# Down projection with VectorE and ScalarE in written order, PSUM banks of even and odd pairs exchanged, and PSUM emptied directly behind each tile

## The chip, the cores and the metric

The kernel runs on one core of one Trainium2 chip. Its time is device microseconds from launch to end; lower is better. One profiled execution gives the trace that is read here. Engines: TensorE (PE in the rows, its weight loads PEld) multiplies matrices into PSUM, VectorE (DVE) and ScalarE (ACT) do elementwise work, GpSimd (POOL) and SyncE (SP) issue transfers, which the DMA engines carry out.

## The reference, cut to what matters

One decoder layer in fp32 on 512 tokens of width 2048: four mixers, an output projection, then the gated MLP and a last norm. The change lies in the MLP's second product, the down projection:

```python
def conv_gated_mlp(h, w_up, w_dw, b_dw, w_down):
    up = h @ w_up
    gate, val = jnp.split(up, 2, axis=-1)
    gate = causal_dwconv(gate, w_dw, b_dw)
    return (jax.nn.gelu(gate, approximate=True) * val) @ w_down
...
        x = x + conv_gated_mlp(h, ffn_w_up[l], ffn_w_dw[l], ffn_b_dw[l], ffn_w_down[l])
    return rmsnorm(x, norm_final_g)
```

`w_down` is 5504 x 2048, so the inner dimension is 43 slices of 128 and the output 16 tiles of 128 columns (d = 0 to 15) by 512 tokens.

## The kernel before, in words

Every fp32 operand is split into a high part `hi` (a ScalarE cast to fp32r) and a low part `lo` (a VectorE subtraction, raw minus hi); a product is two or three matmuls of these parts. So a weight block can be multiplied only after a DMA, a ScalarE cast and a VectorE subtraction, in that order.

`down` works through the 43 slices in four stages, and `down_end` does the last five slices and the norm.

- **Straight stages**, `eights(0)` and `eights(2)`, five slices each. The 16 output tiles are done in two halves of eight (`sw`), and a half takes all eight PSUM banks: tiles d = 0 to 3 in `pb`, d = 4 to 7 in `pa`. One weight chunk (a slice by eight tiles) gives 8 x 3 matmuls. `chunk` stages a chunk's split two chunks ahead (three buffers each for hi and lo). With each of the first seven chunks `forms_dn` prepares, for the next stage, one pair of activation slices (tile `ap`, two buffers, read back from DRAM): three casts on ScalarE, three subtractions and four combinations on VectorE, the last cast waiting for the combinations. After a half the eight banks are emptied: copied to `xn` (stage 0) or added to it (stage 2). The next half needs the banks.
- **Paired stages**, `seven(0)` and `seven(1)`, fourteen slices each, by Winograd's scheme: two by two blocks take seven products instead of eight. For each pair j of output tiles (j and j + 8) there are the products a, r1, r2, b, r3, d, r4 of 14 matmuls, in the order a(j), d(j-1), r1(j), r4(j-1), r2(j), b(j), r3(j). The weight sums r1 and r3 come from an accumulating DMA on POOL. r2 and r4 are made on VectorE in place (r2 = r1 + a, r4 = r2 + b), and only then cast and subtracted. `product` accumulates several forms into one bank (a, r2, r3 and d; r1 and r4), and after every form VectorE adds the bank's two halves to `xn` (two adds of 256 columns). A bank's next form waits for the adds of the form before it. The split of product k + 2 (`stage`) stands in the code ahead of product k and its adds.

What sets the order: TensorE runs in the order of the code. SP and POOL, and before the change VectorE and ScalarE too, are ordered by a scheduler that walks a timeline of its own and lets work of `high_priority` go ahead of other ready work. Each engine then runs its list in order, and an instruction that waits holds up all behind it. `tails` threads the next stage's first loads and splits (`sa`, the activations of a straight stage; `raw`, `hi` and `lo` of its first chunks) into the last seven products.

Of the kernel before, what the change touches and what calls it, by code (L numbers as in the profile page):

```python
# [8 lines left out]
F32 = mybir.dt.float32  # L9
# [4 lines left out]
ADD, SUB, MUL = ALU.add, ALU.subtract, ALU.mult  # L14

P = 128
D = 2048
S = 512
# [31 lines left out]
class Kernel:  # L50
# [1004 lines left out]
    def tail(self):  # L1055
        tc = self.tc
        self.mp.release()
        self.ap.release()
        fx = tc.alloc_tile_pool(name="fx", bufs=1, reuse_waits="tile")
        ft = tc.alloc_tile_pool(name="ft", bufs=1, reuse_waits="tile")  # L1060
        ft2 = tc.alloc_tile_pool(name="ft2", bufs=2, reuse_waits="tile")
        self.x2d = [self.dr.tile([P, 1024], F32, name=f"x2d{p}") for p in range(8)]
        self.tp = ft
        self.acc = self.tmp("rstd", pool=self.cp)
        self.xf = []
        for q in range(4):
            ps = self.quad(q, (0, 2), 0)
            for o in range(4):
                x = self.x2[4 * q + o]
                self.tt(x, x, ps[o], ADD)  # L1070
            for p in (2 * q, 2 * q + 1):
                self.forms1(fx, p)
            for p in (2 * q, 2 * q + 1):
                self.square2(p, ft2)
        self.ffn_std()
        ft2.release()
        ft.release()
        ub = tc.alloc_tile_pool(name="ub", bufs=1, reuse_waits="tile")
        self.ffn_up(self.xf, self.rp, self.rs, ub)
        for pool in (ub, fx, self.aq, self.rp):  # L1080
            pool.release()
        self.rp = tc.alloc_tile_pool(name="rp2", bufs=8, side="right", reuse_waits="tile")
        self.xp = tc.alloc_tile_pool(name="xp", bufs=1, reuse_waits="tile")
        self.fx = tc.alloc_tile_pool(name="fx2", bufs=1, reuse_waits="tile")
        self.ft = tc.alloc_tile_pool(name="ft3", bufs=2, reuse_waits="tile")
        self.down()
        for pool in (self.ft, self.fx):
            pool.release()
        with tc.tile_pool(name="dp", bufs=1, reuse_waits="tile") as dp, \
                tc.tile_pool(name="dp2", bufs=2, reuse_waits="tile") as dp2, \  # L1090
                tc.tile_pool(name="dq", bufs=5, reuse_waits="tile") as self.endq:
            self.tp = dp
            base_tmp = self.tmp
            self.tmp = lambda tag, w=512, dt=F32, pool=None: base_tmp(tag, w, dt, pool or (dp2 if tag == "sq" else None))
            self.down_end()
        for pool in (self.xp, self.rp):
            pool.release()
# [256 lines left out]
    def eights(self, i):  # L1354
        nc, n = self.nc, DN[i + 1] - DN[i]
        forms = list(range(NP2))
        self.xf = []
        step = 0
        for sw in range(2):
            ps = [self.pb() if d < 4 else self.pa() for d in range(8)]  # L1360
            for k in range(n):
                wh, wl = self.chunk()
                if i == sw == 0 and k in (0, 2):
                    self.sacts(i, k + 2, min(k + 4, n))
                for d in range(8):
                    c = slice(d * P, d * P + P)
                    self.mm3(ps[d], wh[:, c], wl[:, c], self.sa[k][:, 0], self.sa[k][:, 1], k == 0, k == n - 1)
                step += 1
                if forms:
                    self.forms_dn(forms.pop(0), DN[i + 1])  # L1370
                if 2 * n - 3 <= step < 2 * n:
                    yield step
            for d in range(8):
                if i == 0:
                    x = self.xp.tile([P, S], F32, tag=f"x{8 * sw + d}", name=f"xn{8 * sw + d}")
                    self.x2.append(x)
                    with self.tc.high_priority(self.hp):
                        nc.scalar.copy(x, ps[d])
                    continue
                x = self.x2[8 * sw + d]  # L1380
                with self.tc.high_priority(self.hp):
                    self.tt(x, x, ps[d], ADD)

    def resid2(self, d):
        x = self.x2d[d // 2][:, 512 * (d % 2):512 * (d % 2) + 512]
# [22 lines left out]
    def seven(self, g):  # L1408
        tc, nc, a = self.tc, self.nc, self.a
        W = NP2 * P  # L1410
        IX = {"a": 0, "b": 1, "r4": 2, "r1": 3, "r3": 4, "d": 5, "r2": 6}
        seq = [(0, x) for x in ("a", "r1", "r2", "b", "r3")]
        for j in range(1, 9):
            for form, back in (("a", 0), ("d", 1), ("r1", 0), ("r4", 1), ("r2", 0), ("b", 0), ("r3", 0)):
                if j - back < 8:
                    seq.append((j - back, form))
        raws, staged, bank = {}, {}, {}
        blk = lambda j, x: a["w_dns"][g, j + 8 * (x in "cd"), :, int(x in "bd")]

        def load(k):  # L1420
            if k >= len(seq):
                return
            j, form = seq[k]
            if form in ("r2", "r4"):
                return
            t = (self.wp if form == "d" else self.rp).tile([P, 1024], F32, tag="raw", name=f"d{form}{g}_{j}")[:, 0:W]
            raws[j, form] = t
            nc.sync.dma_start(t, blk(j, "c" if form in ("r1", "r3") else form))
            if form in ("r1", "r3"):
                nc.gpsimd.dma_start(t, blk(j, "d" if form == "r1" else "a"), accum_op=ADD)  # L1430

        def stage(k):
            if k >= len(seq):
                return
            j, form = seq[k]
            if form in ("r2", "r4"):
                t = raws[j, "r1"]
                self.tt(t, t, raws[j, "a" if form == "r2" else "b"], ADD)
                raws[j, form] = t
            hi = self.wq.tile([P, 1024], F32R, tag="hi", name=f"dh{form}{g}_{j}")[:, 0:W]  # L1440
            lo = self.wq.tile([P, 1024], F32R, tag="lo", name=f"dl{form}{g}_{j}")[:, 0:W]
            self.split_to(hi, lo, raws[j, form])
            staged[k] = (hi, lo)

        def product(k):
            j, form = seq[k]
            wh, wl = staged.pop(k)
            new = form in ("a", "b", "r1")
            if new:
                bank[j, form] = self.pa() if form == "b" else self.pb() if j % 2 else self.pa()  # L1450
            ps = bank[j, {"r2": "a", "r3": "a", "d": "a", "r4": "r1"}.get(form, form)]
            for p in range(NP2):
                x, c = self.xf[p][:, IX[form]], slice(p * P, p * P + P)
                self.mm(ps, wh[:, c], x.rearrange("p n c->p (n c)"), new and p == 0, False, True)
                self.mm(ps[:, 256:512], wl[:, c], x[:, 0], False, p == NP2 - 1, True)
            up, half, op = {"a": (0, 0, ADD), "b": (0, 0, ADD), "r2": (0, 1, ADD), "r4": (0, 1, ADD),
                            "r3": (8, 1, SUB), "r1": (8, 1, SUB), "d": (8, 0, SUB)}[form]
            x = self.x2[j + up][:, 256 * half:256 * half + 256]
            with tc.high_priority(self.hp if k > len(seq) - 4 else 0):
                for i in range(2):  # L1460
                    self.tt(x, x, ps[:, 256 * i:256 * i + 256], op)

        LD, AH = 6, 2
        for k in range(LD):
            with tc.high_priority(self.hp):
                load(k)
        yield None
        for k in range(AH):
            with tc.high_priority(self.hp):
                stage(k)  # L1470
            yield None
        for k in range(len(seq)):
            with tc.high_priority(self.hp):
                load(k + LD)
                stage(k + AH)
            product(k)
            if g == 0 and seq[k][1] == "r3" and seq[k][0] < 6:
                self.resid2(seq[k][0] + 2)
                self.resid2(seq[k][0] + 10)
            yield len(seq) - 1 - k  # L1480
# [139 lines left out]
```

## Time and profile before

| | us |
|---|---|
| median of 3 runs | 1883.13 |
| lowest, highest | 1864.03, 1888.47 |
| the profiled execution | 1867.63 |
| its span, first to last instruction | 1865.8 |
| TensorE busy | 1814.8 (97%) |
| VectorE busy | 1580.3 (85%) |
| ScalarE busy | 908.0 (49%) |

The down projection starts at 1394 us of the span: the first straight stage to 1450, the first paired stage to 1593, the second straight stage to 1655, the second paired stage to 1794, then the end stage. In the rows of a timeline the first number is the start in us, the second the duration; `x2` is two instructions in a row; what stands in brackets is the idle time before it and what ended that. In a list of waits come the total in us, how often, and the longest. Buffer numbers are left out there: `dr` is a raw weight tile of r1 or r3 (and, summed in place, of r2 and r4), `dhr` and `dlr` its high and low part, `da`, `db`, `dd` the tiles of a, b, d; `ap` and `Y` are the activations of a paired stage and their forms.

### The profile page before, as it was taken

Reading aid. Unit: us, or ns where it says so; the run is one execution under the profiler, and the core shown is the slowest. Engines: PE = TensorE matmul, PEld = TensorE weight load, DVE = VectorE, ACT = ScalarE, POOL = GpSimd, SP = SyncE. Lnnn points to the kernel's source line nnn. Section 1 sums busy time; section 2 is a strip of 40 time slices with the busy share of each in tenths; the row PEclk is TensorE's granted clock in tenths of the full one; section 3 lists DMA queues with packets and bytes.
Section 4 is the critical chain, followed back from the end, with each engine's and each line's share of the span. In section 5 each row is a group of like instructions: output and inputs, shape, how many; then the busy total and the mean of one; then the engine's idle time right before and its main releaser. Section 6 shows DMA issues by size and latency. Waiting matters only on the chain.

```text
span 1865.8 us, 26091 instructions
## 1 busy us (share of the span) xinstructions
PE 1814.8 (97%) x9670; PEld 1546.8 (83%) x9670; DVE 1580.3 (85%) x2392; ACT 908.0 (49%) x1188; POOL 208.0 (11%) x291
## 2 busy tenths in 40 slices
PE   8899999999899999999999999999999999899997
PEld 6788887888788888888888888888888788788886
DVE  8699989998695788888888888888887889778975
ACT  6332446533484455555555555555555434433444
POOL 6210020202000100000000000000001210000000
PEclk9999999999999999999999999999999999999998
DMA  5322322423244877777777777777749985577632
GB/s 201 100 88 93 105 94 93 164 80 96 91 167 141 229 212 196 205 202 204 211 194 205 204 202 212 197 206 200 204 120 266 259 209 153 161 213 191 163 99 94
DMA packets 111728, 313.58 MB, mean 168 GB/s; under 512 B 15792, under 2 KB 21936, under 8 KB 111600
## 3 DMA queue, kind: packets, MB, share of 16 engines
q1 hardware_dynamic: 91776, 249.25, 39.6%
q0 software_dynamic: 19536, 62.14, 19.8%
q8 instruction: 76, 1.25, 0.3%
q10 hardware_dynamic: 288, 0.52, 0.1%
q14 instruction: 52, 0.43, 0.1%
HBM read 289.71 MB, written 19.66 MB: 166 GB/s over the span
## 4 chain that ended last, share of the span: by engine, by line
PE 84%; DVE 8%; DMA 4%; ACT 3%; issue 1%; POOL 0%; DVEq 0%; SPq 0%; ACTq 0%; POOLq 0%
PE pa L97 55%; PE pb L97 29%; DVE lo L60 2%; DMA ap<-act 1%; DMA raw<-w_dn 1%; ACT hi L106 1%; DMA ur<-w_up 1%; DVE X L60 1%; DVE M L60 0%; DVE Y L60 0%; DVE A L63 0%; DMA raw<-w_a 0%; DVE bk L60 0%; DVE xn L60 0%; DMA av<-act 0%
## 5 line engine op out<-in xcount | busy, mean ns | idle before, releaser
L97 PE MATMUL pa<-A,hi 128*128 128x512 f32 x1312 | 415.1, 399 | 15.1 <-ACT A L73 7.4
L97 PEld LDWEIGHTS pa<-A,hi 128*128 128x128 f32 x1312 | 247.9, 191 | 75.2 <-ACT A L73 7.8
L106 ACT CAST uhr<-ur 128x1024 fp32r<-128x1024 f32 x160 | 167.9, 1050 | 217.4 <-PE pb L97 112.6
L97 PE MATMUL pa<-A,lo 128*128 128x512 f32 x656 | 258.7, 398 | 2.7 <-DVE lo L60 2.7
L106 ACT CAST hi<-raw 128x1024 fp32r<-128x1024 f32 (+1 forms) x127 | 132.3, 1043 | 219.0 <-PE pa L97 166.4
L60 DVE TENSOR_TENSOR ulr<-ur,uhr 128x1024 fp32r<-128x1024 f32 x160 | 195.8, 1224 | 45.5 <-ACT uhr L106 41.7
L97 PE MATMUL pb<-X,uhr 128*128 128x512 f32 x640 | 225.5, 391 | 1.2 <-ACT uhr L106 1.2
L97 PE MATMUL pa<-X,uhr 128*128 128x512 f32 x640 | 225.4, 391 | 0.0
L60 DVE TENSOR_TENSOR lo<-raw,hi 128x1024 fp32r<-128x1024 f32 (+1 forms) x127 | 157.4, 1241 | 52.4 <-ACT hi L106 51.8
L97 PE MATMUL pb<-X,ulr 128*128 128x256 f32 x640 | 179.3, 280 | 0.8 <-DVE ulr L60 0.8
L97 PE MATMUL pa<-X,ulr 128*128 128x256 f32 x640 | 179.2, 280 | 0.0
L1225 POOL DMA_DIRECT2D ur<-w_up x80 | 69.9, 874 | 802.7 <-DMA ur<-w_up 497.5
L97 PEld LDWEIGHTS pa<-A,lo 128*128 128x128 f32 x656 | 124.6, 190 | 32.1 <-DVE lo L60 3.6
L97 PEld LDWEIGHTS pb<-X,uhr 128*128 128x128 f32 x640 | 119.7, 187 | 27.7 <-ACT uhr L106 1.5
L97 PEld LDWEIGHTS pa<-X,uhr 128*128 128x128 f32 x640 | 119.7, 187 | 26.2
L97 PEld LDWEIGHTS pb<-X,ulr 128*128 128x128 f32 x640 | 121.0, 189 | 1.1 <-DVE ulr L60 1.1
L97 PEld LDWEIGHTS pa<-X,ulr 128*128 128x128 f32 x640 | 121.0, 189 | 0.0
L97 PE MATMUL pa<-X,uhb 128*128 128x512 f32 x320 | 112.7, 391 | 0.0
L106 ACT CAST dhr<-dr 128x896 fp32r<-128x896 f32 x64 | 60.4, 943 | 98.9 <-PE pa L97 51.0
L97 PE MATMUL pa<-X,ulb 128*128 128x256 f32 x320 | 89.6, 280 | 0.0
L63 DVE SCALAR_TENSOR_TENSOR M<-h,par,M 128x511 f32<-128x511 f32 (+29 forms) x120 | 85.7, 747 | 0.1
L97 PE MATMUL pb<-sa,hi 128*128 128x512 f32 (+1 forms) x280 | 77.3, 362 | 4.0 <-DVE xn L60 3.8
(346 smaller groups left out, 4211.6 us busy)
## 6 DMA issues: line engine op xcount, KB each, us to landing
ur<-w_up SPq DMA_DIRECT2D x80, 512.0 KB, 7.7
ur<-w_up POOLq DMA_DIRECT2D x80, 512.0 KB, 7.9
raw<-w_b SPq DMA_DIRECT2D x40, 512.0 KB, 3.7
ud<-w_up SPq DMA_DIRECT2D x40, 512.0 KB, 9.0
ua<-w_up SPq DMA_DIRECT2D x40, 512.0 KB, 7.3
ub<-w_up SPq DMA_DIRECT2D x40, 512.0 KB, 4.3
raw<-w_out SPq DMA_DIRECT2D x32, 512.0 KB, 3.6
dr<-w_dns SPq DMA_DIRECT2D x32, 448.0 KB, 4.1
```

Of the source, the lines that this page charges most:

```text
L60: (eng or self.nc.vector).tensor_tensor(out, x, y, op=op)
L63: self.nc.vector.scalar_tensor_tensor(out, x, s, y, op0=op0, op1=op1)
L97: self.nc.tensor.matmul(ps, lhsT=l, rhs=r, start=start, stop=stop, skip_group_check=go_on)
L106: self.nc.scalar.copy(hi, src)
L1225: nc.gpsimd.dma_start(v8(t), blk(f, "d" if form == "r1" else "a"), accum_op=ADD)
```

## The change

Three things: the whole of `down` is traced with VectorE and ScalarE (and TensorE, as already) in the order of the code; the emptying of a bank stands directly behind its last matmul in the code, and in the first straight stage copies of odd tiles go to VectorE, of even tiles to ScalarE (all were on ScalarE); in the paired stages the banks of a and r1 are `pb` for even j and `pa` for odd j (they were the other way round). SP and POOL stay with the scheduler.

```diff
+        with tc.manual_schedule(engines={mybir.EngineType.PE, mybir.EngineType.DVE, mybir.EngineType.Activation}):
+            self.down()
...
+                    if k == n - 1:
+                        self.empty(i, 8 * sw + d, ps[d])
...
-            for d in range(8):
-                if i == 0:
...
+    def empty(self, i, d, ps):
+        with self.tc.high_priority(self.hp):
+            if i:
+                self.tt(self.x2[d], self.x2[d], ps, ADD)
+                return
+            x = self.xp.tile([P, S], F32, tag=f"x{d}", name=f"xn{d}")
+            self.x2.append(x)
+            if d % 2:
+                self.nc.vector.tensor_copy(x, ps)
+            else:
+                self.nc.scalar.copy(x, ps)
...
-                bank[j, form] = self.pa() if form == "b" else self.pb() if j % 2 else self.pa()
+                bank[j, form] = self.pa() if form == "b" or j % 2 else self.pb()
```

Three places of the engines' lists show what moves. The first is VectorE in the steady part of the first paired stage. `dr10_2` is the raw tile of form r1, stage 0, pair 2; `dlr10`, `dlr20`, `dlr40` are the low parts of r1, r2 and r4; `xn9` is output tile 9. Before:

```order
L60 TENSOR_TENSOR dlr10_2_13631<-dr10_2_13539,dhr10_2_13630 128x896
L60 TENSOR_TENSOR dr10_2_13539<-dr10_2_13539,da0_2_13492 128x896
L60 TENSOR_TENSOR xn2_13133<-xn2_13133,pa884_13634 128x256
L60 TENSOR_TENSOR dlr40_1_13655<-dr10_1_13379,dhr40_1_13654 128x896
L60 TENSOR_TENSOR xn2_13133<-xn2_13133,pa884_13634 128x256
L60 TENSOR_TENSOR xn9_13341<-xn9_13341,pb881_13475 128x256 x2
L60 TENSOR_TENSOR dlr20_2_13678<-dr10_2_13539,dhr20_2_13677 128x896
L60 TENSOR_TENSOR dr10_2_13539<-dr10_2_13539,db0_2_13603 128x896
```

The same place now:

```order
L60 TENSOR_TENSOR dlr10_2_13633<-dr10_2_13541,dhr10_2_13632 128x896
L60 TENSOR_TENSOR xn2_13106<-xn2_13106,pb884_13636 128x256 x2
L60 TENSOR_TENSOR dr10_1_13381<-dr10_1_13381,db0_1_13446 128x896
L60 TENSOR_TENSOR dlr40_1_13657<-dr10_1_13381,dhr40_1_13656 128x896
L60 TENSOR_TENSOR xn9_13325<-xn9_13325,pa881_13477 128x256 x2
L60 TENSOR_TENSOR dr10_2_13541<-dr10_2_13541,da0_2_13494 128x896
L60 TENSOR_TENSOR dlr20_2_13680<-dr10_2_13541,dhr20_2_13679 128x896
L60 TENSOR_TENSOR xn10_13330<-xn10_13330,pb885_13683 128x256 x2
```

Before, other work stood between a weight sum (`dr10 <- dr10, da0` or `db0`) and the low part made from it; now the low part stands directly behind its sum, and ScalarE's cast of that sum lies between the two.

The second place is ScalarE at the change of halves in the first straight stage, where `hi6` is the high part of chunk 6, `Y5_3` form 3 of the next stage, and `xn0` to `xn7` the copies that empty the banks. Before:

```order
L106 CAST hi6_13086<-raw6_13085 128x1024
L1378 COPY xn0_13129<-pb862_12887 128x512
L1378 COPY xn1_13131<-pb863_12888 128x512
L1378 COPY xn2_13133<-pb864_12889 128x512
L1378 COPY xn3_13135<-pb865_12890 128x512
L1378 COPY xn4_13137<-pa866_12891 128x512
L106 CAST Y5_2_13028<-ap5_2_13027 128x4x256
L1378 COPY xn5_13139<-pa867_12892 128x512
L1378 COPY xn6_13141<-pa868_12893 128x512
L106 CAST hi7_13154<-raw7_13153 128x1024
L1378 COPY xn7_13143<-pa869_12894 128x512
L106 CAST Y5_3_13072<-ap5_3_13071 128x256
```

Now:

```order
L106 CAST Y5_3_13074<-ap5_3_13073 128x256
L106 CAST Y5_3_13074<-ap5_3_13073 128x2x256
L106 CAST Y5_3_13074<-ap5_3_13073 128x4x256
L106 CAST hi6_13088<-raw6_13087 128x1024
L1388 COPY xn0_13096<-pb862_12889 128x512
L1388 COPY xn2_13106<-pb864_12891 128x512
L1388 COPY xn4_13116<-pa866_12893 128x512
L1388 COPY xn6_13126<-pa868_12895 128x512
```

The copies stood ahead of all of form 3 and are now behind it; xn1, xn3, xn5 and xn7 stand at the same place in VectorE's list, behind form 3 and the low part of chunk 6.

The third place is VectorE at the end of the first paired stage: `xn15` takes r1, r3 and d of pair 7, `xn7` r4; `dlr40_7` is the low part of r4, `sa23` an activation of the next stage, `lo10` and `lo11` low parts of its chunks. Before:

```order
L60 TENSOR_TENSOR dld0_7_14550<-dd0_7_14444,dhd0_7_14549 128x896
L60 TENSOR_TENSOR xn7_13143<-xn7_13143,pb899_14427 128x256
L60 TENSOR_TENSOR xn7_13143<-xn7_13143,pa901_14553 128x256 x2
L60 TENSOR_TENSOR dlr40_7_14579<-dr10_7_14334,dhr40_7_14578 128x896
L60 TENSOR_TENSOR xn15_13353<-xn15_13353,pb899_14427 128x256 x2
L60 TENSOR_TENSOR lo10_14599<-raw10_14527,hi10_14598 128x1024
L60 TENSOR_TENSOR xn15_13353<-xn15_13353,pb899_14427 128x256 x2
L60 TENSOR_TENSOR lo11_14619<-raw11_14575,hi11_14618 128x1024
L60 TENSOR_TENSOR Y24_0_14681<-ap24_0_14680,Y24_0_14681 128x256
L60 TENSOR_TENSOR Y24_0_14681<-ap24_0_14680,Y24_0_14681 128x2x256
L60 TENSOR_TENSOR Y24_1_14725<-ap24_1_14724,Y24_1_14725 128x256
L60 TENSOR_TENSOR xn7_13143<-xn7_13143,pb900_14481 128x256
```

Now:

```order
L60 TENSOR_TENSOR dld0_7_14552<-dd0_7_14446,dhd0_7_14551 128x896
L60 TENSOR_TENSOR xn7_13131<-xn7_13131,pa901_14555 128x256 x2
L60 TENSOR_TENSOR sa23_14574<-av23_14572,sa23_14574 128x512
L60 TENSOR_TENSOR dr10_7_14336<-dr10_7_14336,db0_7_14400 128x896
L60 TENSOR_TENSOR dlr40_7_14581<-dr10_7_14336,dhr40_7_14580 128x896
L60 TENSOR_TENSOR xn15_13355<-xn15_13355,pa899_14429 128x256 x2
L60 TENSOR_TENSOR lo10_14601<-raw10_14529,hi10_14600 128x1024
L60 TENSOR_TENSOR xn15_13355<-xn15_13355,pa899_14429 128x256 x2
L60 TENSOR_TENSOR lo11_14621<-raw11_14577,hi11_14620 128x1024
L60 TENSOR_TENSOR xn7_13131<-xn7_13131,pa900_14483 128x256 x2
```

The sum for r4 and the activation `sa23` were done well ahead and now stand directly in front of the adds of r3 (the first `xn15`); the adds of r4 (`xn7`, last) had forms of the next stage ahead of the first and, further down, more forms and the low part of chunk 12 ahead of the second, and now stand together.

More of the change, by code (lines that the diff above doesn't have):

```diff
@@ L1085, in tail @@
         self.ft = tc.alloc_tile_pool(name="ft3", bufs=2, reuse_waits="tile")
-        self.down()
+        with tc.manual_schedule(engines={mybir.EngineType.PE, mybir.EngineType.DVE, mybir.EngineType.Activation}):
+            self.down()
         for pool in (self.ft, self.fx):
@@ L1372, in eights @@
                     yield step
-            for d in range(8):
-                if i == 0:
[L1375 to L1382, printed above, removed]
+    def empty(self, i, d, ps):
[9 more added lines that the diff above has]
+                self.nc.scalar.copy(x, ps)
     def resid2(self, d):
```

## The prediction

> **What bounds the kernel now.** I read the page first, then TensorE's waits from 1380 us on (the down projection runs from 1394 to 1794).
>
> ```profile
> span 1865.8 us, 26091 instructions
> PE 1814.8 (97%) x9670; PEld 1546.8 (83%) x9670; DVE 1580.3 (85%) x2392; ACT 908.0 (49%) x1188; POOL 208.0 (11%) x291
> PE pb L97 <- DVE xn L60: 3.8, 1, 3.8
> PE pa L97 <- ACT xn L1378: 3.1, 1, 3.1
> ```
>
> TensorE is busy 97% of the span and nothing in the change alters its matmuls, so time can only go where it stops now, and come where new stops arise. Stops now in the down projection: the joints between its stages. The chain of waits gives the lengths to measure by (first two rows), the windows the first joint and a steady period, TensorE's timeline the start of both straight stages and the second and third joint.
>
> ```profile
> 1501.25 2.43 PE pb L97 x14
> 1633.23 2.75 PE pb L97 x12
> 1449.80:1459.70 9.90, 6.73 (x28) 5.56 (x28) 9.23 (x14) 7.38 (x14) 6.25 (x7) 0.83 0.95 213
> 1453.00:1458.00 5.00, 5.00 (x20) 4.29 (x21) 4.42 (x7) 3.99 (x6) 4.50 (x5) 0.66 1.00 181
> 1501.25:1518.24 16.99, 16.99 (x99) 14.86 (x99) 15.12 (x23) 6.60 (x8) 1.75 (x2) 1.00 0.89 225
> 1394.17 0.63 PE L97 MATMUL pb<-sa,hi 128*128 128x512 f32 x2
> 1593.02 0.63 PE L97 MATMUL pb<-sa,hi 128*128 128x512 f32 x2
> 1599.06 1.19 PE L97 MATMUL pb<-sa,hi 128*128 128x512 f32 x2 [3.80 <-DVE xn L60]
> 1604.31 0.69 PE L97 MATMUL pa<-sa,hi 128*128 128x512 f32 x2
> 1655.66 0.47 PE L97 MATMUL pa<-Y,dha 128*128 128x512 f32 x1 [0.46 <-DVE xn L60]
> ```
>
> A product of a paired stage is 14 matmuls in 2.43; 12 matmuls of a straight stage take 2.75, so a chunk of 24 takes 5.5. A period of seven products takes 17.0, and in it VectorE (third pair of figures) is already busy 15.1. First joint: 9.90 for two products (4.9), 5.0 lost, of it 3.1 by the wait and the rest at a clock of 0.66. Second joint, three tiles into the second straight stage: 3.8 waiting, then four tiles of three matmuls take from 1599.06 to 1604.31, 5.25 instead of 2.75: 6.3 lost. The third loses 0.5. Together 11.8: all that the joints could give back.
>
> **The change part by part.** *The weight sums (a cost).* VectorE and ScalarE around one period:
>
> ```profile
> 1501.29 0.88 DVE L60 TENSOR_TENSOR xn<-xn,pa 128x256 f32<-128x256 f32 x2 [0.47 <-PE pa L97]
> 1502.15 1.09 DVE L60 TENSOR_TENSOR dlr<-dr,dhr 128x896 fp32r<-128x896 f32 x1
> 1503.27 1.09 DVE L60 TENSOR_TENSOR dr<-dr,da 128x896 f32<-128x896 f32 x1
> 1504.61 1.08 DVE L60 TENSOR_TENSOR dlr<-dr,dhr 128x896 fp32r<-128x896 f32 x1
> 1505.61 0.42 DVE L60 TENSOR_TENSOR xn<-xn,pb 128x256 f32<-128x256 f32 x1
> 1506.07 0.94 ACT L106 CAST dhr<-dr 128x896 fp32r<-128x896 f32 x1 [1.53 <-DVE xn L60]
> 1507.05 1.09 DVE L60 TENSOR_TENSOR dlr<-dr,dhr 128x896 fp32r<-128x896 f32 x1
> ```
>
> Two adds take 0.86 (1501.29 to 1502.15), a low part 1.00 to the next instruction (1504.61 to 1505.61), a sum 1.09, a cast 0.94. Now the r2 sum at 1503.27 is followed by other work and its low part comes at 1507.05, the cast hidden between. In the new list nothing stands between sum and low part: VectorE waits out the cast. What the chain of waits has between a cast that ends at 1436.95 and the low part made from it at 1436.97 is the hand-over between the engines:
>
> ```profile
> 1436.95 0.02 issue
> ```
>
> I take 0.03. Let E be the end of product a(j). Adds of a at E+0.04, sum r4 E+0.90 to 1.99, cast to 2.96, low part 2.99 to 4.08; adds of d from 3.99, sum r2 4.85 to 5.94, cast to 6.91, low part 6.94 to 8.03. TensorE reaches r4 at E+4.86 (ready) and r2 at E+7.28; its first low matmul is due 0.23 later, at 7.51, and can start at 8.03 plus 0.14 (start-up, below) = 8.17: late by 0.66. The next five steps (adds 0.86, low part 1.00) give back 5 x 0.57, so VectorE is level again before the next period and the stop recurs. Seven pairs (r4, r2) a stage, two stages: 14 x 0.66 = **+9.2**. Bounds: 0.4 each (5.6) if hand-overs overlap, 0.95 each (13.3) if every add takes its full row.
>
> *The end of a paired stage (a cost).* Five activations `sa` are woven in, 0.60 of VectorE each. They are present now; in the new list they stand at fixed places, two before the last r2 sum, two before the low part of r3, one before the r4 sum.
>
> ```profile
> 1564.15 0.69 DVE L60 TENSOR_TENSOR sa<-av,sa 128x512 fp32r<-128x512 f32 x1
> 1564.76 0.41 DVE L60 TENSOR_TENSOR xn<-xn,pa 128x256 f32<-128x256 f32 x1
> 1587.06 0.88 DVE L60 TENSOR_TENSOR xn<-xn,pb 128x256 f32<-128x256 f32 x2 [0.71 <-PE pb L97]
> 1588.08 0.47 PE L97 MATMUL pb<-Y,dhd 128*128 128x512 f32 x1 [1.06 <-ACT hi L106]
> ```
>
> The last two rows are d(7): it follows r3(7) in the same bank, so it waits 1.06 for r3's adds (they end 1587.94, TensorE resumes 0.14 later; the cast that the row names ended about then too, but d does not read it). New walk, same E for a(7): r2 late by 0.66 + 1.20; adds of r2 start only at 14.06, behind two `sa` and r3's low part, so r3 starts at 15.04 where b ended at 13.99 (+1.05); then low part of d, adds of b, `sa`, and the whole sum-cast-low chain of r4, 3.1, stand ahead of r3's adds, which end at 21.4; r3 ended at 17.5, so d waits 4.0 where it waits 1.06 (+2.9). Per stage 1.20 + 1.05 + 2.9 = 5.2; two stages **+10.3** (bounds 6 to 13, with or without the r3 stop and with a late `av` load).
>
> *Change of halves, first straight stage (a cost).* Each chunk's step on VectorE is now form, then low part, in line.
>
> ```profile
> 1402.40 0.42 DVE L60 TENSOR_TENSOR Y<-ap,Y 128x256 fp32r<-128x256 f32 x1
> 1433.88 0.69 DVE L60 TENSOR_TENSOR Y<-ap,Y 128x512 fp32r<-128x512 f32 x1 [1.93 <-ACT Y L106]
> 1435.40 0.89 DVE L63 SCALAR_TENSOR_TENSOR ap<-ap 128x256 f32<-128x256 f32 x2
> 1436.84 1.05 ACT L106 CAST Y<-ap 128x1024 fp32r<-128x1024 f32 x1
> 1436.97 1.23 DVE L60 TENSOR_TENSOR lo<-raw,hi 128x1024 fp32r<-128x1024 f32 x1 [0.69 <-ACT hi L106]
> 1438.11 1.22 DVE L60 TENSOR_TENSOR Y<-ap,Y 128x1024 fp32r<-128x1024 f32 x1
> 1412.72 2.63 DMA av<-act
> 1417.19 8.69 DMA ap<-act
> ```
>
> First split 0.34, then 1433.88 to 1436.29, the cast with hand-overs 1.11, the last split 1.13: a form is 5.0; with the low part (1.14) 6.1, against 5.5 of TensorE. And the copies that empty the banks stand behind form 3. Walk: form 0 starts at 1402.4 and ends 1409.3, with three instructions of the up projection between (estimated as 0.6 each, like the 512-wide split at 1433.88, which lets the next start 0.6 later); low part, form 1, low part to 1416.6; one `sa`. Form 2 needs a buffer that form 1 frees at 1415.4 and then a load, behind three weight loads that SP now issues ahead of it: between 2.6 and 8.7 by the chain's two rows, I take 6. Its second half is cast by 1422.1, so form and low part end near 1427.9, form 3 near 1432.9, and the first copy, behind form 3's cast and chunk 6's high part on ScalarE, near 1433.3. TensorE is through its half at 1394.2 + 5 x 5.5 + 0.3 = 1421.9: 11.4 of waiting, and 2.5 at half clock as at the second joint. The remaining five chunks then run on; the paired stage starts 54.9 + 0.3 + 11.4 + 2.5 = 69.1 after 1394.2, without a stop. Now its first two products end at 1459.7, as if begun 60.7 after: **+8.4**, the first joint's gain included (bounds +5 and +12 for the two loads).
>
> [...]
>
> *Second straight stage (a gain).* The second joint goes: r4's two adds are no longer parted by a low part that waited for a load, and the banks are exchanged so that `pb`, needed first, is free.
>
> ```profile
> 1597.36 1.23 DVE L60 TENSOR_TENSOR lo<-raw,hi 128x1024 fp32r<-128x1024 f32 x1 [1.50 <-ACT hi L106]
> 1598.50 0.41 DVE L60 TENSOR_TENSOR xn<-xn,pb 128x256 f32<-128x256 f32 x1
> 1589.28 6.90 DMA raw<-w_dn
> ```
>
> But four forms of 6.1 lie ahead of the half's adds: if chunk 12's load lands as now (1596.2), the forms start at 1598.5, the first add ends 1623.8, TensorE was ready at 1620.5: 3.3 lost and up to 1.7 of slow clock. If it lands 3 earlier, 1.0 and none. The stage takes 62.6 now (1593.0 to 1655.66) and would take 56 to 60: between -7.7 and -2.7, **-5.0**; the third joint is in it.
>
> *Copies on VectorE.* No trace row shows them. Nearest: VectorE's add out of PSUM of the same size and ScalarE's copies.
>
> ```profile
> L60 DVE TENSOR_TENSOR xn<-xn,pa 128x512 f32<-128x512 f32 x12 | 7.9, 684 | 0.0
> L1378 ACT COPY xn<-pa 128x512 f32<-128x512 f32 x8 | 4.6, 631 | 0.0
> ```
>
> Between 0.63 and 0.68 each, four of them running beside ScalarE's four: 0 in the sum, since TensorE fills a tile in 0.69; without the cover 8 x 0.65 = 5. [...]
>
> *Queues.* SP issues weight loads in another order (d before b) and POOL's residual loads move later; 0, since loads wait for buffers and not the reverse; if that cover fails, see the third rival.
>
> **Sum:** 9.2 + 10.3 + 8.4 - 5.0 = +22.9. The profiled execution took 1867.6 (span 1865.8 and 1.8 around it), so 1890.5; but that execution is 15.5 under the median. The four known times (1864.0, 1867.6, 1883.1, 1888.5) average 1875.8, which is the fairest base: **1899**.
>
> **The rivals.** *The lead covers the chains (faster than now).* Splits run two products or two chunks ahead. If every chain in line were some 10% shorter than I walk it, r2's low part would be in time (0.33 off each of two chains of 3.95) and a form with its low part would keep up with a chunk (6.1 to 5.5), so that VectorE never falls behind, and only the joints change: -11.8, 1855.8 from the profiled time, 1864 from the base. For it: VectorE is idle 1.9 of a period now. Against it: two exposed casts take 2 x 1.0, all of that. 0.17.
>
> *Nothing measurable.* Stops at the ends and at the first change of halves are shorter, because loads land early, and won and lost cancel: 0 to +10, 1876 to 1886. 0.13.
>
> *Loads become late.* Strict order frees weight buffers later, and SP waits for them already:
>
> ```profile
> SPq L1428 <- DVE xn L60: 55.2, 18, 4.8
> ```
>
> If a load misses by 1.5 once a period, 14 periods add 21: +44, 1920. For it: 18 such waits in 120 us; against: the period above, 17.0 and TensorE busy all of it. 0.10.
>
> **How the numbers follow.** Forecast 0.60; all its low bounds give 5.6 + 6 + 5 - 7.7 = +9, all its high ones 13.3 + 13 + 12 - 2.7 = +36. On bases of 1866 to 1886 that is 1875 to 1922; the first two rivals pull the low end to 1868, the third the high end to 1924, and about 0.2 stay outside. Two per cent of the median, about what a measurement can tell from no change, is 1845.5 and 1920.8: slower takes the top of the forecast (0.04) and half or more of the late loads (0.07), faster only a low base under the cover rival (0.02).
>
> **What would show it.** Right: `dlr` waiting for ACT `dhr` about 14 times or more by 1.0 at a sum; TensorE stops of 0.7 once a period before r2, of 4 before d(7); one stop near 10 at about 1422; none where the joints at 1450 and 1595 are now. Wrong: periods still 17.0; no stop at 1422 (copies early, forms short); VectorE waiting for `dr` or `da` loads.

## The result and the profile after

The changed kernel takes 1894.2 us (median of 16 runs, 1890.1 to 1908.5), the kernel before on the same chip 1874.0 (16 runs, 1864.0 to 1888.5). The ratio is 1.0121, 95% interval 1.0095 to 1.0148: slower, by less than 2%. The prediction was 1899, and 22.9 over a base of 1875.8, which is a ratio of 1.0122. The profiled execution took 1891.9, 24.3 more than that of before. Two of the ten executions of e9 below took 3009 and 3646 where the others took 1861 to 1882; medians and ratios leave them out.

The page of the kernel after, and TensorE's waits from 1380 us on (total, times, longest):

```profile
span 1890.1 us, 26057 instructions
PE 1823.8 (96%) x9670; PEld 1552.0 (82%) x9670; DVE 1583.6 (84%) x2400; ACT 900.4 (48%) x1180; POOL 208.2 (11%) x291
PE pb L97 <- ACT xn L1388: 8.3, 1, 8.3
PE pa L97 <- DVE xn L60: 7.6, 3, 3.7
PE pa L97 <- DVE dlr L60: 4.3, 8, 0.6
PE pb L97 <- DVE dlr L60: 3.2, 6, 0.6
PE pa L97 <- ACT dhr L106: 2.0, 2, 1.2
```

The two joints that stood here before (3.1 and 3.8) are gone. In their place are fourteen stops of some 0.5 for the low part of r2 (the `dlr` rows), one of 8.3 for ScalarE's first copy, three of 7.6 in all for VectorE's adds at the ends of the paired stages, and there two of 2.0 in all for ScalarE's cast of r2 (`dhr`). No row names a weight load. TensorE's timeline gives the starts of the stages and the stops before d(7):

```profile
1393.79 0.62 PE L97 MATMUL pb<-sa,hi 128*128 128x512 f32 x2
1429.77 1.22 PE L97 MATMUL pb<-sa,hi 128*128 128x512 f32 x2 [8.35 <-ACT xn L1388]
1459.25 0.39 PE L97 MATMUL pb<-Y,dha 128*128 128x512 f32 x1
1603.41 0.47 PE L97 MATMUL pa<-Y,dhd 128*128 128x512 f32 x1 [3.68 <-DVE xn L60]
1609.91 0.63 PE L97 MATMUL pb<-sa,hi 128*128 128x512 f32 x2
1665.63 0.40 PE L97 MATMUL pb<-Y,dha 128*128 128x512 f32 x1
1810.54 0.77 PE L97 MATMUL pa<-Y,dhd 128*128 128x512 f32 x1 [3.19 <-DVE xn L60]
1818.07 0.63 PE L97 MATMUL pb<-sa,hi 128*128 128x512 f32 x2
```

The same starts read from every profiled execution give one table, in us from a stage's first matmul to the next stage's. All kernels but the first two are the experiments below; "sums" is in all from e3 on except e4 and e12.

| kernel | first straight | first paired | second straight | second paired | together |
|---|---|---|---|---|---|
| before | 58.7 | 140.2 | 62.6 | 138.2 | 399.7 |
| after | 65.5 | 150.7 | 55.7 | 152.4 | 424.3 |
| e1 order alone | 72.1 | 151.2 | 63.1 | 149.8 | 436.1 |
| e2 moves alone | 57.8 | 148.1 | 57.3 | 142.7 | 405.9 |
| e3 sums earlier | 66.1 | 140.8 | 55.9 | 143.0 | 405.8 |
| e4 form 3 behind the copies | 62.7 | 153.1 | 55.3 | 151.5 | 422.6 |
| e5 activations on GpSimd | 66.2 | 143.2 | 55.7 | 141.3 | 406.5 |
| e6 low part inside the form | 67.7 | 142.8 | 55.9 | 140.8 | 407.2 |
| e7 order from the paired stage on | 56.9 | 149.3 | 56.2 | 141.4 | 403.8 |
| e8 all of e3 to e6 | 66.9 | 143.3 | 57.0 | 143.5 | 410.8 |
| e10 adds first at the end | 68.0 | 137.9 | 60.6 | 140.1 | 406.5 |
| e11 all with other buffers | 57.8 | 139.6 | 61.0 | 140.0 | 398.4 |
| e12 ScalarE left to the planner | 76.1 | 152.0 | 58.8 | 151.0 | 438.0 |

The up projection ahead of `down` starts it between 1391 and 1410 us, whatever the kernel (last section), so single stages are compared here rather than spans.

One period of the changed kernel, on VectorE:

```profile
1546.23 0.88 DVE L60 TENSOR_TENSOR xn<-xn,pa 128x256 f32<-128x256 f32 x2 [0.48 <-PE pa L97]
1547.02 1.08 DVE L60 TENSOR_TENSOR dr<-dr,db 128x896 f32<-128x896 f32 x1
1549.19 1.09 DVE L60 TENSOR_TENSOR dlr<-dr,dhr 128x896 fp32r<-128x896 f32 x1 [1.08 <-ACT dhr L106]
1550.98 1.09 DVE L60 TENSOR_TENSOR dr<-dr,da 128x896 f32<-128x896 f32 x1
1553.15 1.09 DVE L60 TENSOR_TENSOR dlr<-dr,dhr 128x896 fp32r<-128x896 f32 x1 [1.08 <-ACT dhr L106]
```

Both sums show the exposed cast, 1.08 each time. VectorE's next instruction behind the second low part starts at 1554.16, and TensorE's timeline has its first low matmul of r2 0.14 after that:

```profile
1554.30 0.39 PE L97 MATMUL pa<-Y,dlr 128*128 128x256 f32 x1 [0.61 <-DVE dlr L60]
```

And the windows, of the second end in the kernel before and in the one after (columns: busy time of PE, PEld, DVE, ACT, POOL, then granted clock, DMA share, GB/s):

```profile
1777.54:1793.82 16.28, 15.22 (x86) 12.82 (x85) 12.90 (x21) 5.87 (x6) 0.00 (x0) 1.00 0.21 65
```

```profile
1586.88:1609.91 23.03, 17.27 (x86) 14.09 (x85) 17.26 (x27) 8.06 (x10) 0.90 (x1) 0.93 0.56 171
1793.54:1818.07 24.53, 19.51 (x86) 16.16 (x85) 17.43 (x27) 8.05 (x10) 0.00 (x0) 0.79 0.18 54
```

The same six products, r4(6) to r4(7), take 16.3 before and 23.0 and 24.5 after, partly by stops and partly because the clock falls to 0.93 and 0.79.

### The profile page after: what moved, and what is told of

It reads as the page before. It is cut to its first block, busy times and chain, and to the rows that moved or that the text cites. A ratio compares the mean times of both kernels' runs of the same rounds, so it can differ in the third digit from the quotient of the medians.

```text
span 1890.1 us, 26057 instructions
## 1 busy us (share of the span) xinstructions
PE 1823.8 (96%) x9670; PEld 1552.0 (82%) x9670; DVE 1583.6 (84%) x2400; ACT 900.4 (48%) x1180; POOL 208.2 (11%) x291
## 4 chain that ended last, share of the span: by engine, by line
PE 81%; DVE 11%; ACT 3%; DMA 2%; issue 2%; SPq 0%; POOL 0%; ACTq 0%; DVEq 0%; POOLq 0%
PE pa L97 53%; PE pb L97 28%; DVE dlr L60 2%; DVE xn L60 2%; ACT dhr L106 2%; DVE dr L60 2%; DVE lo L60 1%; DMA ur<-w_up 1%; DMA ap<-act 1%; DVE M L60 0%; DVE X L60 0%; DMA par<-par 0%; DVE bk L60 0%; DVE sa L60 0%; DVE pr L60 0%
## 5 line engine op out<-in xcount | busy, mean ns | idle before, releaser
L60 DVE TENSOR_TENSOR dlr<-dr,dhr 128x896 fp32r<-128x896 f32 x64 | 69.7, 1090 | 35.0 <-ACT dhr L106 35.0
```

The costliest lines, as they stand in the source:

```text
L60: (eng or self.nc.vector).tensor_tensor(out, x, y, op=op)
```

## The experiments

Theory: chains in VectorE's line make the loss (at the sums, at the two ends, at the change of halves), and the moves of copies and banks give the joints back. Ratios are to the kernel before on the same chip.

**e3, the sums one step earlier.** The sum for r2 and r4 is written behind the stage before, ahead of the adds of a product:

```diff
                 stage(k + AH)
+                total(k + AH + 1)      # the sum, taken out of stage
             product(k)
```

> The changed kernel, with each weight sum of r2 and r4 written one step earlier, ahead of the adds of the product before, so that one pair of adds (0.87) stands between a sum and its low part. Theory (the exposed cast of 1.0 is what makes r2 late): the stops of 0.5 to 0.6 before r2's low part go in all 12 periods (-9.5) and each end loses 1 to 2 less: about 1882. Rival (VectorE's load as such sets the pace, 15 of 17 us and two waits that only show it): the wait moves to another instruction, periods stay near 17.9, 1894. Rival (the sums now wait for loads in their earlier place): periods over 18, above 1896.

Measured: 1874.9, ratio 1.0029 (0.9992 to 1.0065), where the changed kernel has 1.0121. All fourteen `dlr` stops are gone, and both paired stages are 9.4 to 9.9 shorter. VectorE in the same place of a period:

```profile
1546.96 1.09 DVE L60 TENSOR_TENSOR dlr<-dr,dhr 128x896 fp32r<-128x896 f32 x1 [0.30 <-ACT dhr L106]
1547.97 1.08 DVE L60 TENSOR_TENSOR dr<-dr,da 128x896 f32<-128x896 f32 x1
1548.97 0.87 DVE L60 TENSOR_TENSOR xn<-xn,pb 128x256 f32<-128x256 f32 x2
1550.14 1.09 DVE L60 TENSOR_TENSOR dlr<-dr,dhr 128x896 fp32r<-128x896 f32 x1 [0.30 <-ACT dhr L106]
```

The adds now run beside the cast, and the wait falls from 1.08 to 0.30. VectorE's work is the same, so it was the chain and not the load. That the two stages gain 19 and not 12 says that the ends, too, were late by these chains.

**e1 and e2, the two halves of the change apart.** e1 puts `down` under the written order and leaves copies and banks as they were; e2 has the moves and no order.

```diff
+        with tc.manual_schedule(engines={PE, DVE, Activation}):     # e1 alone
+            self.down()
...
+                        self.empty(i, 8 * sw + d, ps[d])            # e2 alone, with the banks
```

> The order as written on VectorE and ScalarE alone; banks and copies stay where they were before the change. Theory (the order costs at the weight sums, the ends of the paired stages and the change of halves; the moves of copies and banks give some of it back): each pair (r4, r2) shows VectorE waiting about 1.0 at both sums and r2's product 0.7 to 0.9 long, as in the changed kernel; the ends lose 7 to 8 each, too. The copies now stand behind one form more (5.0 later) and the joints stay as before (5.0 and 6.3): 15 to 20 over the changed kernel, about 1911. Rival (the moves of copies and banks are what costs, the order is free): periods of 17.0 and about 1874. Rival (order alone is all of the cost and the moves give nothing back): 1894.

> Banks exchanged and copies and adds directly behind their tile, but VectorE and ScalarE keep the planner's order. Theory: periods of 17.0 and ends as before the change; the first joint loses less than its 5.0 (half of the copies are on VectorE, the bank needed first is free) and the second less than its 6.3: 1862 to 1872, about 1867. Rival (the moves are what costs): 1885 or more. Rival (the moves do nothing without the order): 1874.

e1: 1900.3, ratio 1.0151 (1.0085 to 1.0217); its down projection is 11.8 longer than the changed kernel's, short of the 15 to 20 foreseen. The pair stops are there (0.46 to 0.61), the stop at the first change of halves is 14.7 instead of 8.35, and the second straight stage has one of 4.5. So the order costs some 36 of the down projection and the moves give 12 back. No joint stop appeared in it: the first paired stage is as long as in the changed kernel.

e2: 1876.3, ratio 1.0020 (0.9985 to 1.0055), not the 1867 that the theory gave. Periods have no stop (17.3 at its 2.47 a product), and the second straight stage is 5.3 shorter, as foreseen; but the time comes back one product later. TensorE's timeline of e2, at the first and at the second paired stage:

```profile
1458.73 0.80 PE L97 MATMUL pb<-Y,dhr 128*128 128x512 f32 x1 [3.91 <-DVE Y L60]
1661.72 0.77 PE L97 MATMUL pb<-Y,dhr 128*128 128x512 f32 x1 [2.82 <-DVE xn L60]
```

Behind the bank stood the next wait: r1(0) for the last form's split, and r1 of the second stage for adds. So without the order the moves gain nothing that was measured.

**e12, ScalarE left to the planner**, VectorE as written.

> The changed kernel, but ScalarE is left to the planner: order as written on TensorE and VectorE alone. Theory (all the costs are chains in VectorE's line): stops as in the changed kernel, 0.5 to 0.6 before r2 in every period, over 3 before d(7); at the change of halves ScalarE's copies come early, so TensorE gets one tile further and then waits for VectorE's first copy, 7 to 8: within 3 of the changed kernel, about 1894. Rival (ScalarE's place in line costs as much: the high part of chunk 6 and form 3's cast stand before its copies): 8 to 11 less, about 1884.

1912.5, ratio 1.0184 (1.0116 to 1.0252): neither theory. The paired stages are those of the changed kernel, stop for stop (0.46 to 0.61 before r2, 3.65 before d(7)), so these are VectorE's. But the first straight stage takes 76.1. The timelines of ScalarE and VectorE there:

```profile
1432.28 1.04 ACT L106 CAST hi<-raw 128x1024 fp32r<-128x1024 f32 x1 [3.24 <-DMA raw<-w_dn]
1434.30 1.23 DVE L60 TENSOR_TENSOR Y<-ap,Y 128x1024 fp32r<-128x1024 f32 x1 [4.70 <-ACT Y L106]
1442.13 0.43 DVE L60 TENSOR_TENSOR Y<-ap,Y 128x256 fp32r<-128x256 f32 x1 [4.87 <-ACT Y L106]
```

ScalarE's own list has other casts, and the waits for their loads, ahead of the cast that VectorE's fixed list needs next. Two lists made by two rules wait for each other; the stage takes 10.6 more than under the written order on both and 17.4 more than under the planner's.

**e5 and e10, the ends.** In e3 d(7) still waits 2.5 in each stage, behind the fifth activation and r4's low part. e5 takes VectorE's load away; e10 changes the place, of r4's low part and of the fifth activation:

```diff
-                self.split_to(t[:, 0], t[:, 1], r[:, c])
+                self.split_to(t[:, 0], t[:, 1], r[:, c], eng=gpsimd if i else None)     # e5
...
-            if left in (7, 5, 3):
+            if left in (7, 5, 2):                                               # e10: the fifth activation later
...
-                stage(k + AH)
+                if k != len(seq) - 3: stage(k + AH)                                     # e10: for r3(7)
             product(k)
+            if k == len(seq) - 3: stage(k + AH)                                         # its adds first
```

> The kernel with the sums one step earlier, and the low parts of the five activations at the end of each paired stage computed on GpSimd instead of VectorE. Theory (the ends are VectorE's load: it works without a gap there, and 3.1 of it are these five): the remaining stops of 2.5 before d(7) fall to about the 1.06 that was there before the change and no longer bring a low clock: 3 to 4.5 less in each end, about 1867. Rival (the place in line of r4's chain ahead of r3's adds makes the stop, not the load): stops of 2 or more stay, 1875. Rival (GpSimd is late with them, or slows VectorE beside it): the second straight stage or the tail starts with a new stop, 1875 or more.

> The kernel with the sums one step earlier, and at the end of each paired stage r3's adds ahead of the low part of r4, with the fifth activation behind both. Theory (d(7) waits for what stands ahead of r3's adds: 0.7 of activation and 1.1 of low part): the stops of 2.5 before d(7) fall to about 1.0 and leave the clock alone, 3 less in each end: about 1869. Rival (VectorE is behind by its whole load at the end, whatever the order): r3 or r4 wait instead, the ends stay as long, 1875.

e5: 1887.1, ratio 1.0047 (1.0004 to 1.0091). The stops stay (2.61 and 2.56). GpSimd and VectorE in its timeline:

```profile
1594.51 3.72 POOL L60 TENSOR_TENSOR sa<-av,sa 128x512 fp32r<-128x512 f32 x2 [11.11 <-ACT sa L106]
1594.90 2.18 DVE L60 TENSOR_TENSOR dr<-dr,da 128x896 f32<-128x896 f32 x1
1599.97 1.85 DVE L60 TENSOR_TENSOR dlb<-db,dhb 128x896 fp32r<-128x896 f32 x1
```

Beside GpSimd's 1.86 each, a sum of 1.08 took 2.18 and a low part of 1.08 took 1.85: most of what VectorE was spared (five low parts of 0.6) it lost again. What slows VectorE beside GpSimd is not shown by any run here. The experiment therefore leaves load and place undecided.

e10: 1879.2, ratio 1.0024 (0.9987 to 1.0061). The place decides: d(7) waits 1.06 in both stages, as in the kernel before, and the paired stages are 2.9 shorter each, some 1.4 by the stop and the rest by the slow clock that followed it in e3, where d(7) and r4(7) took 6.50 instead of 4.86 in the first. But the time is e3's, since the second straight stage is 4.7 longer (and the first, which the edit does not touch, 1.9). In e10's timeline TensorE waits at that stage's change of halves, and ScalarE shows why:

```profile
1641.72 1.19 PE L97 MATMUL pb<-sa,hi 128*128 128x512 f32 x2 [4.09 <-DVE xn L60]
1614.16 1.05 ACT L106 CAST hi<-raw 128x1024 fp32r<-128x1024 f32 x1 [5.46 <-DMA raw<-w_dn]
```

The four forms, 6.1 each, begin behind chunk 12's high part, which waits for its load until 1614.16; in e3 it was cast 0.7 after the stage began, here 4.2 after. Counted from the start of the paired stage that cast came at 141.5 in e3 and at 142.0 in e10: it kept its time, while the stage ended 2.9 sooner. So the stage's adds end when that load and four forms let them, and TensorE, coming sooner, waits: what the end gained, the transfer behind it took.

**e4, e6, e8, e9, the first change of halves.** e4 (on the changed kernel) writes form 3 behind the fifth chunk; e6 (on e3) writes the next chunk's low part into the form, ahead of its last split; e8 has e3, e5, e4's and e6's edits together.

```diff
-                if forms:
+                if forms and not (i == 0 and step == 4):                    # e4, e8, e9
...
         self.stt(g, h, -1.0, g, MUL, SUB)
+        if i == 0: self.stage_upto(min(self.used + AHEAD, self.limit))      # e6, e8, e9
         self.split_to(x[:, 3:7, 0], x[:, 3:7, 1], v)
```

> The changed kernel, with form 3 of the first straight stage written behind the fifth chunk and its copies instead of ahead of them. Theory (the copies stand behind form 3 in line): they follow form 2 and the low part of chunk 6, so TensorE, through its half at about 1421, waits some 2.4 instead of 8.35 and keeps its clock; the forms behind then end near the start of the paired stage and may cost 0 to 2 there: the first straight stage takes 57 to 60 instead of 65.5, the time is about 1887. Rival (late loads of activations set the stop, not the place in line): the stop stays at 6 or more, 1892 to 1894. Rival (the form's delay comes back whole at the start of the paired stage): the stop goes and one of 5 or more appears at about 1450, 1893.

> The kernel with the sums one step earlier, and in the first straight stage the low part of the next chunk written inside each form, between its last difference and its last split, so that the form's cast (1.1) runs beside it. Theory (the chain form, cast, split, low part in line is what puts the copies late): about 1.1 gained in each of the first forms, the stop at the change of halves falls from 8.7 to 5 to 6 and the stage from 66 to about 63: 1871. Rival (the load of form 2 sets it): the stop stays above 7.5, 1874. Rival (VectorE's whole load sets it): the stop stays at 8.7, 1875.

> Sums one step earlier, low parts of the five activations on GpSimd, chunk's low part inside each form of the first straight stage, and form 3 behind the copies. Theory: every part of the cost of the order is hidden: first straight stage about 57, paired stages about 138 each, second straight stage 56: some 9 and 8 below the kernel with the sums alone, about 1858, under the kernel before. Rival (costs return elsewhere, as forms late at the first joint): 1866 to 1875.

e4: 1902.5, ratio 1.0127 (1.0067 to 1.0187), no gain. The stop falls from 8.35 to 4.62, not to 2.4, and a new one of 2.33 before r2(0), behind which the product takes 2.50, so without a slow clock, takes most of the 2.7 that the stage gained back: half of the rival that it comes back whole. e6: 1879.3, ratio 1.0026 (0.9984 to 1.0068), no gain over e3; the stop grew to 9.85. e8: 1880.8, ratio 1.0019 (0.9980 to 1.0059); the stop is 7.14. What held e6 stands in its timeline:

```profile
1414.84 1.81 SPq L1400 DMA_DIRECT2D ap<-act  x4
1421.80 0.41 ACT L106 CAST Y<-ap 128x256 fp32r<-128x256 f32 x1 [7.54 <-DMA ap<-act]
1422.24 0.42 DVE L60 TENSOR_TENSOR Y<-ap,Y 128x256 fp32r<-128x256 f32 x1 [6.82 <-ACT Y L106]
```

The forms had become shorter (5.0 a chunk), and then VectorE stood 6.8 for form 2's activations. Their load is issued only when form 1 has left its buffer, because one of the stage's own activations took the other, and by then three weight loads are under way. The rival of e6, the load, was right. So e9 gives that activation another pool:

```diff
-            r = rp.tile(...) if fs[0] == 0 else ft.tile(...)
+            r = rp.tile(...) if i == 0 else ft.tile(...)
```

> As the kernel with all parts, but the low parts of the end stay on VectorE, and the activations of the first straight stage's own chunks are loaded into buffers of another pool, so that the two buffers of the forms are the forms' alone and form 2's load can be issued a form earlier. Theory (with the forms' chain shortened, what holds the change of halves is form 2's load, 6.8 to 7.5 of VectorE's waiting, taken behind three weight loads): the wait goes, the copies come near TensorE's own end of the half, the stop falls from 7.1 to under 2.5 and the first straight stage from 66.9 to 58 to 60: about 1868. Rival (the DMA engines are full there whatever the buffer; it lands no earlier): the stop stays at 6 or more, 1875. Rival (form 3 and later ones are now late for the paired stage): the stop goes, and one of 3 or more stands at the first joint.

1872.3, the median of eight, ratio 0.9998 (0.9956 to 1.0040). The profiled execution was the one of 3009, so its stop can't be read; e11 contains the same edit and shows it.

**e7, the order from the first paired stage on**, the first straight stage left to the planner, with the sums earlier.

> The kernel with the sums one step earlier, and the order as written from the end of the first straight stage on only; that stage keeps the planner's order. Theory (the first straight stage's stop comes from the order alone): no stop at the change of halves, the stage takes about 58 instead of 66, a stop of 2 to 4 returns at the joint behind it, with a low clock: 4 to 5 of the 8 stay, about 1870. Rival (the exchanged banks and moved copies make that stop): it stays, 1875.

1881.4, ratio 1.0043 (1.0007 to 1.0078), no better than e3, though the down projection is 2.0 shorter (1.6 of that in the second paired stage, where a stop of 2.48 before d(7) happened to bring no slow clock: the product behind it took 2.51; last section). The stop at the change of halves is gone, as the theory says; behind the joint r1(0) waits for the last form, 4.52 after 1.75, and the product behind it takes 4.09 instead of 2.43 (4.65 behind e2's 3.91): e2's stop again. So the written order moves that stage's wait, and the planner pays it later.

**e11, all that hid a chain**: e3, e4's and e6's edits, e10, e9's buffer, and the same other buffer for the fifth activation of an end.

> All parts that hide a chain, together: sums one step earlier, r3's adds ahead of r4's low part, the chunk's low part inside each form of the first straight stage, form 3 behind the copies, and other buffers for that stage's own activations and for the fifth one of each end, so that the forms' two buffers are theirs. Theory (each stop was a chain in VectorE's line or a form's load behind it): d(7) waits 1.06, paired stages 138 and 140, first straight stage 58 to 60, the second 56 and without the stop of 4.1 that the late fifth activation brought: 392 to 395 for the down projection where the kernel before takes 399.7, so 5 to 8 under it: about 1864 by its median here. Rival (form 2's load is late whatever its buffer): the first straight stage stays at 65 or more, equal to the kernel before. Rival (the stop at the second change of halves does not hang on that buffer): 60 there, 1868.

1863.7, ratio 0.9967 (0.9932 to 1.0002): the fastest here, though the interval still holds no change. TensorE's waits in the down projection of e11:

```profile
PE pb L97 <- DVE xn L60: 4.5, 2, 3.2
PE pa L97 <- DVE xn L60: 2.4, 3, 1.1
PE pb L97 <- ACT xn L1389: 1.8, 1, 1.8
```

No stop stands at the first change of halves (57.8 for the stage). e8, which in that stage differs by e9's buffer alone, has 7.14: so what was left there after the edits of e4 and e6 hung on form 2's load. The joint waits 1.8 and 1.3, d(7) 1.06. The second straight stage keeps a stop of 3.2 and takes 61.0: the rival was right that this does not hang on the fifth activation's buffer.

## Why the prediction was right

The size and the sign came out, by terms that were partly wrong. That the sums agree to the tenth is luck: the ends cost 4.7 more than predicted, the change of halves 3.6 less, and the second straight stage gave 1.9 more. From the two traces, against the prediction's sum:

| term | predicted | measured | how |
|---|---|---|---|
| weight sums | +9.2 | +9.4 | 12 periods by 0.70 to 0.91 |
| ends of the paired stages | +10.3 | +15.0 | (23.03 - 16.23) + (24.53 - 16.28) |
| change of halves and first joint | +8.4 | +4.8 | first paired stage begins 65.5 after the start, 60.7 in effect before |
| second straight stage | -5.0 | -6.9 | 55.7 against 62.6 |
| start of the second paired stage | 0 | +0.6 | stop of 0.35 |
| sum | +22.9 | +22.9 | |

The spans differ by 24.3; `down` starts 0.4 earlier after, and of its 91 undisturbed products 47 run at 2.47 instead of 2.43, where before it was 10 of 104: 37 by 0.045 is the other 1.7.

- **Weight sums.** The mechanism is shown by e3. Each r2 is 0.79 longer on average where 0.66 was worked out; twelve of the fourteen stand in the periods, the last of each stage in its end. So part of the agreement in this row is bookkeeping: all fourteen at 0.79 would be 11.1.
- **Ends.** The mechanism is shown by e3 and e10, the size was missed. Stops between products came to 5.8 and 5.0, less 1.06 each of before: 8.7, less than foreseen. What the sum left out is the clock behind them: 6.3 of the 15.0 (behind the 3.68 two products took 6.50 at a granted clock of 0.74, behind the 3.19 one took 4.62 at 0.50). The prediction charged the stop at the change of halves 2.5 for this and the stops before d(7), of the same kind, nothing. It is a price that need not come (last section): in e1 a stop of 3.15 before d(7) left the clock at 1.00.
- **Change of halves.** The stop is 8.35 instead of 11.4 and the slow clock 2.2 (four tiles in 4.92 at a granted clock of 0.58, instead of 2.75) instead of 2.5. The mis-sized step is form 2's load, taken as 6: it landed 3.7 after its issue, by SP's and ScalarE's timelines of the kernel after:

```profile
1413.70 0.80 SPq L1400 DMA_DIRECT2D ap<-act  x2
1417.37 0.41 ACT L106 CAST Y<-ap 128x256 fp32r<-128x256 f32 x1 [3.48 <-DMA ap<-act]
```

  With 3.7 in the walk the stop comes to 9.1. How much hangs on this load showed only in e6 and e11.
- **Second straight stage.** Its two joints went, as foreseen; the stop of 1.0 to 3.3 at its change of halves did not come. e10 says why: with the ends as long as they are after, chunk 12's load lands in time; where the ends are shorter still, the stop is there (4.1). e1, without the banks exchanged, has no stop at the second joint either, and e2, without the order, keeps 1.2: the order alone removes it. The slow clock set beside the longer stop, up to 1.7, agrees with the first joint before, where 5.00 at a clock of 0.66 lose 1.70; that a stop of 1.0 brings none agrees with the 1.06 before d(7), behind which two products took 4.94 at 1.00.
- **First joint.** No stop, as foreseen. e1 has none there either, without the banks exchanged, and e2 with them has 2.3: it is the order, which brings TensorE late, that removes it.
- **The rivals.** The lead does not cover the chains: twenty-one stops of the down projection are against it. "Nothing measurable" fails by the interval. No weight load stopped TensorE in the changed kernel; loads decide only once the chains are shortened.

The base was good fortune as well as reason: the average of the four known times, 1875.8, lies 2 over the median of sixteen.

## What to carry to other kernels

In a list that runs as written, put independent work between a step and the step of the same engine that waits for another engine's answer: here one line moved by one place brought back three quarters of a 1.2% loss. Price a stop with the slow clock that may follow it, some 1.7 here, and not with its length alone. And before shortening a chain at a stage's end, look at the transfer that the next stage starts with: two of the gains here (e6, e10) were taken back by a load.

## What was not expected of the hardware

**The clock behind a stop is nearly all or nothing, and its length does not settle which.** Windows of TensorE's first product after a stop of 1.78 (e11), from a stop of 1.96 (e8) and after one of 3.15 (e1); the granted clock is the third number from the end:

```profile
1464.83:1467.40 2.57, 2.57 (x14) 2.25 (x15) 2.54 (x4) 1.69 (x4) 1.84 (x3) 1.00 1.01 259
```

```profile
1459.25:1463.36 4.11, 4.11 (x15) 3.53 (x16) 4.08 (x7) 2.34 (x4) 3.12 (x4) 0.58 1.07 253
```

```profile
1822.82:1825.36 2.54, 2.54 (x14) 2.21 (x15) 0.99 (x1) 0.00 (x0) 0.00 (x0) 1.00 0.25 40
```

After 1.06 and 1.78 the product cost 0.1 more than 2.43. After 1.96 it cost 1.7 more at a clock of 0.58, after 2.47 (e3) and 3.68 (the changed kernel) two products cost 1.6 more. But behind stops of 2.33 (e4), 2.48 (e7), 2.56 (e8) and 3.15 (e1, at 1.00) the product took 2.50 to 2.54. Pairs of stops a microsecond apart differ in the same way: behind 1.20 and 0.63 in the second end of the changed kernel the product that they fall in took 1.8 more than its 2.43 and the second stop, behind 0.90 and 0.62 in e1 1.9 more, and behind 1.05 and 0.62 in e4, at the same place, 0.4 more. So between 1.96 and 3.15 a stop may bring the slow clock or not, and a stage of a single trace carries some 1.7 of chance for each such stop. No run here varies one property of a stop by itself, and what decides stays open.

**TensorE has two paces at a granted clock of 1.00.** The same stretch of the up projection, which no kernel here changes, before and in e11:

```profile
700.00:800.00 100.00, 100.00 (x579) 1.00 0.75 199
```

```profile
700.00:800.00 100.00, 100.00 (x568) 1.00 0.74 198
```

579 matmuls against 568 in 100 us, without a wait in either. The traces of after and of e10 show the same two counts. It goes with a start of `down` near 1394 or near 1406, some 12 apart, which is half the range of the kernel before's own times (1864 to 1888) and as much as separates the medians of e3 and e11. The lowest times, which by the author's estimate depend less on it, put e11 (1861.1) 1.6 under the kernel before on its chip (1862.7). Why one or the other pace is taken is open.
